# Starting an expert's first products inside the preceding expert, and its biases as two float32r parts

## Chip, cores, metric

One core of a Trainium2 chip runs the whole program. The metric is the device time of one execution in microseconds; the time of the kernel is the median of its runs. The engines are named as in the profile: PE is TensorE (PEld its weight loads), DVE VectorE, ACT ScalarE, POOL GpSimd; SP is the engine that issues most transfers.

## What is computed

Two transformer blocks on 256 tokens of width 1024, in float32. The first has a token mixer of two recurrent branches and then a mixture of 32 experts; the second has attention and a dense feed-forward part. The change is in the experts. Each token goes to its 4 best experts of 32, and what each expert computes is:

```python
gu = xb @ w_gu[e] + b_gu[e]
glu = jnp.minimum(gu[:, :D_EXPERT], SWIGLU_LIMIT)
lin = jnp.clip(gu[:, D_EXPERT:], -SWIGLU_LIMIT, SWIGLU_LIMIT)
act = glu * jax.nn.sigmoid(SWIGLU_ALPHA * glu) * (lin + 1.0)
return (act @ w_down[e] + b_down[e]) * p[:, None].astype(h.dtype)
```

`w_gu[e]` is 1024 x 2048 and `w_down[e]` 1024 x 1024, so an expert reads 12.58 MB of weights, and the 32 experts 402.7 MB.

## The kernel before

The experts run one after the other, over all 32, each with room for 64 tokens (`CAP`). An overflow path, `over`, runs for experts with more tokens; it is a branch that stands behind expert 30.

**Weights.** `moe` lists all 384 chunks of 1 MB in the order of their use: for each expert eight gate/up chunks (128 rows of `w_gu`), then four down chunks (256 rows of `w_down`), at L1177 to L1183. They go through a ring of 16 slots (`K.rings`). `load_to` (L1186) issues the next load on SP's queue; the first 16 are issued ahead, during the merge, and from then on the use of one chunk asks for the load of one more, which waits until the slot it falls on has been read.

**One expert** (`expert`, L1289). `biases(e)` (L1277) takes the two PSUM banks `pg` and `pl` (two buffers each), has POOL spread a selecting pattern `se`, and starts the accumulation with two float32 products of `se` and the bias table `bgu`. Then come the eight gate/up chunks (L1298): the 64 tokens are the stationary operand, the weights move, and each bank takes two half-width products, one in partitions 0 to 63 and one in 64 to 127. A float32 product is two instructions in the trace, so a chunk is eight and the biases are four. `expert_act` (L1219) computes the activation on DVE and ACT from both banks; `act_T` (L1231) transposes its result on PE (L1234) and ACT copies it out (L1236); then the four down chunks (L1309) accumulate in `po`, and DVE scales the result (L1317).

**Between the experts.** Every second expert gathers the tokens of the next pair (`gather`, L1242, products at L1261) and combines an earlier pair into the output (`combine`, L1319, products at L1339). Expert 1's own gather is the rest of the generator `g0`, run behind expert 0.

**Order.** The order in which the code is written is not the order on an engine: the framework's scheduler puts each engine's instructions in a row, within the data dependencies, and only a few are pinned (`issue_after`, `keep_in_program_order`). All SP transfers stand in one queue in their order of issue.

**Constants.** `route_consts` (L1056), during the merge, loads the router's weights, the bias tables and index rows by POOL's queue. `split` (L48) makes a high and a low float32r part of a float32 tile, with a copy on ACT and a subtraction on DVE (L49, L50); the merge's weights go through it, too, and are multiplied in three float32r products each (L76 to L78).

Of the kernel before, what the change touches and what calls it, by code (L numbers as in the profile page):

```python
# [7 lines left out]
F32 = mybir.dt.float32  # L8
# [7 lines left out]
P = 128  # L16
# [1032 lines left out]
NE = 32  # L1049
CAP = 64  # L1050

COMBINE = {e: [(e - 3, e - 2)] for e in range(3, 30, 2)}
COMBINE.update({30: [(28, 29), (30,)], 31: [(31,)]})


def route_consts(K, rc):  # L1056

    nc, I = K.nc, K.I
    def bank():
        return K.psum.tile([P, 512], F32, name="mod", bufs=1)  # L1060
    post_vecs(K, rc, bank)
    wr = rc.tile([P, 8, NE], F32, name="wr")
    nc.gpsimd.dma_start(wr, I["w_router"].rearrange("o (k p) e -> p (o k) e", p=P))
    br = rc.tile([P, NE], F32, name="br")
    bcast_rows(nc, nc.gpsimd, br, I["b_router"], NE)
    bgu = rc.tile([P, 512], F32, name="bgu")
    for q in range(4):
        nc.gpsimd.dma_start(bgu[q * NE:(q + 1) * NE, :], I["b_gu"][0, :, q * 512:(q + 1) * 512])
    bdn = rc.tile([P, 512], F32, name="bdn")
    for q in range(2):  # L1070
        nc.gpsimd.dma_start(bdn[q * 64:q * 64 + NE, :], I["b_down"][0, :, q * 512:(q + 1) * 512])
    iof = rc.tile([P, 256], F32, name="iof")
    nc.gpsimd.iota(iof, pattern=[[1, 256]], base=0, channel_multiplier=0, allow_small_or_imprecise_dtypes=True)
    ups = rc.tile([P, P], F32, name="ups")
    nc.vector.tensor_sub(ups, K.upT, K.ident)

    sel = rc.tile([P, NE, 2], F32, name="sel")
    ih = K.ident.rearrange("p (i h e) -> p i e h", i=2, h=2)
    nc.vector.tensor_add(sel, ih[:, 0], ih[:, 1])
    pb = bank()  # L1080
    for k in range(8):
        nc.tensor.matmul(pb[:, :NE], K.sh2c[:, k:k + 1].to_broadcast([P, P]), wr[:, k, :], start=(k == 0), stop=(k == 7))
    nc.vector.tensor_add(br, pb[:, :NE], br)
    K.rc = wr, br, bgu, bdn, iof, ups, sel


class router:


    def __init__(self, K, rc, psum, mp):  # L1090
        self.K, self.nc, self.rc, self.psum, self.mp = K, K.nc, rc, psum, mp

        def T(name, *shape, dt=F32):
            return rc.tile([P, *shape], dt, name=name)
        self.lg, self.m8, self.idx, self.idf = T("lg", 2, NE), T("top", 2, 8), T("idx", 2, 8, dt=U32), T("idf", 2, 8)
        self.A, self.slot, self.Pw, self.ps = T("A", 2, NE), T("slot", 2, NE), T("Pw", 2, NE), T("ps", 2)
        self.eq, self.rs2 = T("eq", 2, 4, NE), T("rs2", 2)
        self.cnt, self.cmax = T("cnt", NE + 1, dt=I32), T("cmax", 1)
        self.pl = psum.tile([P, 512], F32, name="po", bufs=1)
        self.pc = psum.tile([P, 512], F32, name="tr", bufs=1)  # L1100
        self.h2T = [mp.tile([P, 8, P], F32, name="xT", bufs=2) for _ in range(2)]
# [25 lines left out]
    def top(self, t):  # L1127
        K, nc, lg, A = self.K, self.nc, self.lg[:, t, :], self.A[:, t, :]
        _, br, _, _, iof, _, _ = K.rc
        nc.vector.scalar_tensor_tensor(lg, self.pl[:, t * NE:(t + 1) * NE], self.rs2[:, t:t + 1], br, op0=OP.mult, op1=OP.add)  # L1130
        nc.vector.max(out=self.m8[:, t, :], in_=lg)
        nc.vector.max_index(out=self.idx[:, t, :], in_max=self.m8[:, t, :], in_values=lg)
        nc.vector.tensor_copy(self.idf[:, t, :], self.idx[:, t, :])
        nc.vector.tensor_tensor(self.eq[:, t], iof[:, None, :NE].to_broadcast([P, 4, NE]),
                                self.idf[:, t, :4, None].to_broadcast([P, 4, NE]), op=OP.is_equal)
        return nc.vector.tensor_reduce(A, self.eq[:, t].rearrange("p j e -> p e j"), axis=mybir.AxisListType.X, op=OP.add)

    def count(self):
        K, ups = self.K, self.K.rc[5]
# [26 lines left out]
def moe(K, rc, dbg=None):  # L1166
# [10 lines left out]
    wq = {}  # L1177
    chunks = []
    for e in range(NE):
        for k in range(8):  # L1180
            chunks.append((e, "gu", k))
        for k in range(4):
            chunks.append((e, "dn", k))  # L1183
    nload = [0]
# [57 lines left out]
    def gather(g):  # L1242

        S = mp.tile([P, 2, 2, CAP], F32, name="S", bufs=2)
        SP = mp.tile([P, 2, 2, CAP], F32, name="SP", bufs=1)
        xT = mp.tile([P, 8, 2, CAP], F32, name="xT", bufs=2)
        xTs[g] = xT
        for e0, e1 in ((0, 1), (1, 2)) if g == 0 else ((0, 2),):
            m = e1 - e0
            for t in range(2):  # L1250
                nc.vector.tensor_tensor(S[:, t, e0:e1], iof[:, None, :CAP].to_broadcast([P, m, CAP]),
                                        slot[:, t, g * 2 + e0:g * 2 + e1, None].to_broadcast([P, m, CAP]), op=OP.is_equal)
            if (g, e0) == (0, 0):
                R.scaled(0, 1)
                R.scaled(1, 1)
            for k4 in range(2):
                p = tr() if g else psum.tile([P, 512], F32, name="y", bufs=2)
                for kk in range(4):
                    for t in range(2):
                        k = k4 * 4 + kk  # L1260
                        nc.tensor.matmul(p[:, kk * P:kk * P + m * CAP], h2[:, t, k * P:(k + 1) * P],  # L1261
                                         S[:, t, e0:e1].rearrange("p e c -> p (e c)"), start=(kk == 0 and t == 0),
                                         stop=(kk == 3 and t == 1), skip_group_check=True)
                nc.scalar.activation(xT[:, k4 * 4:k4 * 4 + 4, e0:e1],
                                     p.rearrange("p (k e c) -> p k e c", k=4, e=2)[:, :, :m], AF.Copy)
            if e0 == 0:
                yield
        w = mp.tile([P, 2, P], F32, name="PwT", bufs=3)
        PwT[g] = w
        for t in range(2):  # L1270
            nc.vector.tensor_mul(SP[:, t], S[:, t], Pw[:, t, g * 2:g * 2 + 2, None].to_broadcast([P, 2, CAP]))
        p = tr()
        for t in range(2):
            nc.tensor.transpose(p[:, t * P:(t + 1) * P], SP[:, t].rearrange("p e c -> p (e c)"), K.ident)
        nc.scalar.activation(w, p[:, :2 * P].rearrange("p (t n) -> p t n", t=2), AF.Copy)

    def biases(e):  # L1277

        pg = psum.tile([P, 512], F32, name="pg", bufs=2)
        pl = psum.tile([P, 512], F32, name="pl", bufs=2)  # L1280
        se = mp.tile([P, 2, CAP], F32, name="se", bufs=2)
        nc.gpsimd.tensor_copy(se, sel[:, e, :, None].to_broadcast([P, 2, CAP]))  # L1282
        for i, pp in enumerate((pg, pl)):
            q = slice(i * 2 * NE, (i + 1) * 2 * NE)
            nc.tensor.matmul(pp, se[q].rearrange("p h c -> p (h c)"), bgu[q, :], start=True, stop=False,  # L1285
                             skip_group_check=True)
        return pg, pl

    def expert(e):  # L1289
        xT = xTs[e // 2][:, :, e % 2, :]  # L1290
        pg, pl = accs.pop(e) if e in accs else biases(e)
        for k in range(8):
            w = wq.pop((e, "gu", k))
            load_to(nload[0] + 1)
            for pp, off in ((pg, 0), (pl, 1024)):
                for half in range(2):
                    hs = slice(half * CAP, (half + 1) * CAP)
                    nc.tensor.matmul(pp[hs, :], xT[:, k, :], w[:, off + half * 512:off + half * 512 + 512],  # L1298
                                     start=False, stop=(k == 7), skip_group_check=True)
        b = expert_act(pg, pl)  # L1300
        aT = act_T(b)
        po = psum.tile([P, 512], F32, name="po", bufs=1)
        for k2 in range(4):
            w = wq.pop((e, "dn", k2))
# [49 lines left out]
    R.weights()  # L1354
    for e in range(NE):
        expert(e)
        if e == 0:
            for _ in g0:
                pass
        if e == 30:  # L1360

            K.ahead = {}
# [14 lines left out]
def over(K, mp, psum, tr, expert_act, act_T, cnt, slot, Pw, iof, add_y):  # L1377
# [4 lines left out]
    with tc.If(m > CAP):  # L1382
        with tc.tile_pool(name="over", reuse_waits="tile", bufs=1) as vp:
            with tc.For_i(0, NE) as e:
                n = nc.values_load(cnt[0:1, bass.ds(e, 1)], min_val=0, max_val=256)
                with tc.If(n > CAP):
                    se = vp.tile([P, 2, 2], F32, name="se")
                    nc.vector.tensor_copy(se[:, :, 0:1], slot[:, :, bass.ds(e, 1)])
                    nc.vector.tensor_copy(se[:, :, 1:2], Pw[:, :, bass.ds(e, 1)])
                    for b in range(1, 4):  # L1390
                        S = vp.tile([P, 2, CAP], F32, name="S")
                        SP = vp.tile([P, 2, 2, CAP], F32, name="SP")
                        for t in range(2):
                            nc.vector.tensor_scalar(S[:, t], iof[:, b * CAP:(b + 1) * CAP], se[:, t, 0:1], None, op0=OP.is_equal)
                            nc.vector.tensor_scalar(SP[:, t], S[:, t, None, :].to_broadcast([P, 2, CAP]), se[:, t, 1:2], None,
                                                    op0=OP.mult)
                        xT = vp.tile([P, 8, CAP], F32, name="xT")
# [595 lines left out]
```

## Time and profile before

| | us |
|---|---|
| median of 3 runs (2106.03 to 2109.7) | 2108.91 |
| profiled execution | 2117.05 |
| its span, first to last instruction | 2115.4 |
| PE busy in the span | 1923.3 |
| experts' gate/up products, first to last start | 766.3 to 1726.9 |

The profile is one execution. Its rows give start and length in microseconds from the span's start. Busy time is a share of the whole span, over stages with different limits; what a stage is worth is read in that stage alone. Matmuls overlap, so a row's length includes the drain of its last one. An idle time in brackets names what ended it.

### The profile page before, as it was taken

The numbers are of one execution on the slowest core, as the hardware profiler recorded it, in microseconds if no ns is written. First come the engines' busy times: TensorE is split into PE (matmuls) and PEld (weight loads), VectorE is DVE, ScalarE is ACT, GpSimd is POOL, SyncE is SP. The second block draws the span as 40 slices with busy tenths as digits, with TensorE's granted clock in tenths as the row PEclk, the third lists the DMA queues.
The fourth block names the chain that finished last, engine by engine and source line by source line (L and its number), as shares of the span: only waits on it lengthen the run. The fifth ranks groups of instructions, "written<-read, shape, count | busy, mean of one in ns | idle before, by whom it ended". The sixth has DMA issues, their size and how long they took to land. (4 is left out here: it accounts for less than half of the span.)

```text
span 2115.4 us, 27709 instructions
## 1 busy us (share of the span) xinstructions
PE 1923.3 (91%) x10742; PEld 1167.0 (55%) x10743; DVE 968.4 (46%) x2244; ACT 652.4 (31%) x1368; POOL 172.6 (8%) x247
## 2 busy tenths in 40 slices
PE   4786979799998999999999999999999889998998
PEld 1664758688986763333333233333333328778997
DVE  2797785866464642221122212111221127667777
ACT  2564555476554410000000000000000004564554
POOL 1342131311102000000000000000000000000000
PEclk8798999898999989999999999999999988998999
DMA  8346654447534789999999999999999963333551
GB/s 259 70 124 205 201 158 100 113 111 205 175 127 164 271 322 404 417 389 417 418 417 416 417 412 416 417 418 418 417 416 417 418 231 123 126 120 100 189 189 41
DMA packets 191938, 569.59 MB, mean 269 GB/s; under 512 B 47919, under 2 KB 90776, under 8 KB 158650
## 3 DMA queue, kind: packets, MB, share of 16 engines
q1 hardware_dynamic: 160064, 507.19, 62.4%
q0 software_dynamic: 13392, 47.72, 7.4%
q10 hardware_dynamic: 18346, 12.86, 2.5%
q8 instruction: 86, 1.41, 0.3%
q14 instruction: 50, 0.41, 0.1%
HBM read 555.22 MB, written 12.50 MB: 268 GB/s over the span
## 5 line engine op out<-in xcount | busy, mean ns | idle before, releaser
L1298 PE MATMUL pg<-w,xT 128*64 128x512 f32 x1024 | 358.3, 600 | 0.0
L1298 PE MATMUL pl<-w,xT 128*64 128x512 f32 x1024 | 352.4, 594 | 0.0
L50 DVE TENSOR_TENSOR wlo<-w,whi 128x1024 fp32r<-128x1024 f32 (+1 forms) x185 | 224.1, 1212 | 137.7 <-ACT whi L49 134.8
L49 ACT ACTIVATE whi<-w 128x1024 fp32r<-128x1024 f32 (+1 forms) x189 | 197.3, 1047 | 213.5 <-PE pj L77 68.5
L1309 PE MATMUL po<-w,aT 128*64 128x512 f32 x1024 | 242.2, 617 | 21.3 <-ACT aT L1236 21.3
L1224 ACT ACTIVATE th<-ga 128x512 f32<-128x512 f32 x32 | 20.2, 631 | 639.2 <-DVE ga L1222 639.2
L1317 DVE TENSOR_TENSOR o<-po,g 64x512 f32<-64x512 f32 x64 | 44.1, 689 | 315.2 <-PE po L1309 314.5
L1222 DVE TENSOR_SCALAR ga<-pg 128x512 f32<-128x512 f32 x32 | 22.1, 692 | 355.7 <-PE pg L1298 355.7
L1298 PEld LDWEIGHTS pl<-w,xT 128*64 128x64 f32 x1024 | 104.2, 137 | 146.2 <-issue 146.1
L1298 PEld LDWEIGHTS pg<-w,xT 128*64 128x64 f32 x1024 | 99.2, 137 | 150.0 <-issue 147.5
L1309 PEld LDWEIGHTS po<-w,aT 128*64 128x64 f32 x1024 | 71.2, 141 | 150.7 <-issue 118.0
L77 PE MATMUL pj<-wlo,hh 128*128 128x256 f32 x384 | 116.6, 304 | 3.6 <-DVE wlo L50 3.3
L76 PE MATMUL pj<-whi,hh 128*128 128x256 f32 x384 | 115.4, 300 | 3.8 <-ACT whi L49 3.8
L78 PE MATMUL pj<-whi,hl 128*128 128x256 f32 x384 | 115.0, 299 | 0.0
L76 PE MATMUL pj<-hh,whi 128*128 128x512 f32 (+1 forms) x264 | 100.7, 383 | 11.8 <-ACT hh L49 9.4
L372 DVE SCALAR_TENSOR_TENSOR acc<-padl,taps,acc 128x256 f32<-128x256 f32 x192 | 106.1, 567 | 9.7 <-ACT acc L365 7.6
L78 PE MATMUL pj<-hh,wlo 128*128 128x512 f32 (+1 forms) x264 | 99.6, 378 | 7.1 <-DVE wlo L50 6.9
L77 PE MATMUL pj<-hl,whi 128*128 128x512 f32 (+1 forms) x264 | 100.5, 381 | 0.1
L77 PEld LDWEIGHTS pj<-wlo,hh 128*128 128x128 f32 x384 | 78.3, 204 | 12.0 <-DVE wlo L50 4.5
L1339 PE MATMUL y<-o,PwT 128*128 128x512 f32 (+1 forms) x136 | 72.1, 639 | 13.7 <-DVE o L1317 10.2
L1282 POOL COPY se<-sel 128x128 f32<-128x128 f32 x32 | 12.2, 382 | 868.5 <-PE pl L1285 812.0
L1217 DVE TENSOR_TENSOR x<-x,y 128x512 f32<-128x512 f32 x68 | 46.5, 688 | 78.2 <-PE y L1339 78.2
(676 smaller groups left out, 3615.3 us busy)
## 6 DMA issues: line engine op xcount, KB each, us to landing
w<-in_w_gu_dram SPq DMA_DIRECT2D x256, 1024.0 KB, 11.3
w<-in_w_down_dram SPq DMA_DIRECT2D x139, 1024.0 KB, 13.2
w<-in_w_in_dram POOLq DMA_DIRECT2D x72, 512.0 KB, 5.6
w<-in_w_mod_dram SPq DMA_DIRECT2D x48, 512.0 KB, 6.1
w<-in_w_up_dram SPq DMA_DIRECT2D x22, 1024.0 KB, 5.1
w<-in_w_in_dram SPq DMA_DIRECT2D x8, 1024.0 KB, 5.2
gbc<-gD ACTq DMA_DIRECT2D x16, 256.0 KB, 6.2
actD<-la ACTq DMA_DIRECT2D x16, 256.0 KB, 5.4
```

The source lines that it names most:

```text
L49: K.nc.scalar.activation(hi, src, AF.Copy)
L50: (lo_eng or K.nc.vector).tensor_sub(lo, src, hi)
L76: nc.tensor.matmul(out, ah, bh, start=first, stop=False, **kw)
L77: nc.tensor.matmul(out, ah, bl, start=False, stop=False, **kw)
L78: nc.tensor.matmul(out, al, bh, start=False, stop=last, **kw)
L372: eng.scalar_tensor_tensor(al, pl[:, dy:dy + 4, dx:dx + 64], w, al, op0=OP.mult, op1=OP.add)
L1217: nc.vector.tensor_add(y[:, t, ds_], y[:, t, ds_], p)
L1222: nc.vector.tensor_scalar(a, pg, 7.0, None, op0=OP.min)
L1298: nc.tensor.matmul(pp[hs, :], xT[:, k, :], w[:, off + half * 512:off + half * 512 + 512], start=False, stop=(k == 7), skip_group_check=True)
L1309: nc.tensor.matmul(po[dh * CAP:(dh + 1) * CAP, :], aT[:, k % 4, (k // 4) * CAP:(k // 4 + 1) * CAP], w[:, kk * 1024 + dh * 512:kk * 1024 + ...
L1317: nc.vector.tensor_mul(outs[e // 2][e % 2 * CAP:(e % 2 + 1) * CAP, dh * 512:(dh + 1) * 512], po[hs], K.g2[hs])
L1339: nc.tensor.matmul(ps[dh], PwT[g][hs, t, :], outs[g][hs, dh * 512:(dh + 1) * 512], start=(g > 0), stop=True)
```

## The change

`chunks` lists the first two gate/up chunks of expert e + 1 ahead of expert e's down chunks, so they are loaded in that order. `expert` is split: `up(e, ks)` does the biases, if they aren't done, and the products of the chunks `ks`. `expert(e)` does its own chunks 2 to 7, calls the activation, then does chunk 0 of expert e + 1, the transposes, chunk 1 of expert e + 1, and the down products. Experts 0 and 31 (`ALONE`) aren't started early. The rest of `g0` runs inside each call, which has an effect in expert 0 only.

The bias table is loaded into a buffer of the `la` tag of another pool, split into float32r parts `bgh` and `bgl`, and each bank gets two float32r products in place of a float32 one; `se` is float32r too. To make room, `iof` shrinks from 256 columns to 64 and `eq` loses its token index; `over` subtracts 64 from the slots per block in place of reading further along `iof`.

```diff
+ALONE = 0, 31
...
-    bgu = rc.tile([P, 512], F32, name="bgu")
+    bgu = K.wsp.tile([P, 512], F32, name="la", bufs=2)
     for q in range(4):
         nc.gpsimd.dma_start(bgu[q * NE:(q + 1) * NE, :], I["b_gu"][0, :, q * 512:(q + 1) * 512])
+    bgh, bgl = (rc.tile([P, 512], F32R, name=n) for n in ("bgh", "bgl"))
+    split(K, bgu, bgh, bgl)
...
-    iof = rc.tile([P, 256], F32, name="iof")
-    nc.gpsimd.iota(iof, pattern=[[1, 256]], base=0, channel_multiplier=0, allow_small_or_imprecise_dtypes=True)
+    iof = rc.tile([P, CAP], F32, name="iof")
+    nc.gpsimd.iota(iof, pattern=[[1, CAP]], base=0, channel_multiplier=0, allow_small_or_imprecise_dtypes=True)
...
-        for k in range(8):
+        for k in range(0 if e in ALONE else 2, 8):
             chunks.append((e, "gu", k))
+        if e + 1 < NE and e + 1 not in ALONE:
+            chunks += [(e + 1, "gu", 0), (e + 1, "gu", 1)]
         for k in range(4):
             chunks.append((e, "dn", k))
...
-        se = mp.tile([P, 2, CAP], F32, name="se", bufs=2)
+        se = mp.tile([P, 2, CAP], F32R, name="se", bufs=2)
         nc.gpsimd.tensor_copy(se, sel[:, e, :, None].to_broadcast([P, 2, CAP]))
         for i, pp in enumerate((pg, pl)):
             q = slice(i * 2 * NE, (i + 1) * 2 * NE)
-            nc.tensor.matmul(pp, se[q].rearrange("p h c -> p (h c)"), bgu[q, :], start=True, stop=False,
-                             skip_group_check=True)
+            for j, part in enumerate(bgu):
+                nc.tensor.matmul(pp, se[q].rearrange("p h c -> p (h c)"), part[q, :], start=(j == 0), stop=False,
+                                 skip_group_check=True)
         return pg, pl
...
-    def expert(e):
+    def up(e, ks):
+
         xT = xTs[e // 2][:, :, e % 2, :]
-        pg, pl = accs.pop(e) if e in accs else biases(e)
-        for k in range(8):
+        if e not in accs:
+            accs[e] = biases(e)
+        pg, pl = accs[e]
+        for k in ks:
             w = wq.pop((e, "gu", k))
             load_to(nload[0] + 1)
...
-        b = expert_act(pg, pl)
+
+    def expert(e):
+
+        up(e, range(0 if e in ALONE else 2, 8))
+        ahead = e + 1 < NE and e + 1 not in ALONE
+        b = expert_act(*accs.pop(e))
+        for _ in g0:
+            pass
+        if ahead:
+            up(e + 1, (0,))
         aT = act_T(b)
+        if ahead:
+            up(e + 1, (1,))
         po = psum.tile([P, 512], F32, name="po", bufs=1)
...
         expert(e)
-        if e == 0:
-            for _ in g0:
-                pass
```

## Rows read from the trace of the kernel before

**Rows 1.** The page: GB/s moved by DMA in 40 equal slices.

```profile
GB/s 259 70 124 205 201 158 100 113 111 205 175 127 164 271 322 404 417 389 417 418 417 416 417 412 416 417 418 418 417 416 417 418 231 123 126 120 100 189 189 41
```

**Rows 2.** Stretches: us, busy (x) of PE, PEld, DVE, ACT, POOL, clock, DMA share, GB/s.

```profile
768.00:805.00 37.00, 37.00 (x194) 17.99 (x192) 7.19 (x15) 3.96 (x8) 0.00 (x0) 0.98 0.93 371
...
900.00:930.00 30.00, 28.88 (x134) 11.60 (x136) 6.50 (x12) 2.81 (x5) 0.37 (x1) 1.00 1.01 378
...
1000.00:1200.00 200.00, 189.35 (x812) 66.98 (x814) 39.99 (x67) 12.70 (x22) 2.46 (x7) 0.99 1.02 417
1200.00:1400.00 200.00, 189.87 (x834) 68.10 (x832) 39.21 (x65) 13.33 (x23) 2.56 (x7) 1.00 1.01 415
1400.00:1600.00 200.00, 190.99 (x848) 69.48 (x846) 37.96 (x64) 13.69 (x24) 2.20 (x6) 1.00 1.02 417
```

**Rows 3.** Waits of the DMA queue, 1000 to 1600 us: total, times, longest.

```profile
SPq L1191 <- PE po L1309: 207.4, 80, 6.8
```

**Rows 4.** Last gate/up load of experts 8 and 30: issue, landing time, products.

```profile
991.02 0.33 SPq L1191 DMA_DIRECT2D w<-in_w_gu_dram  x1
...
w<-in_w_gu_dram SPq DMA_DIRECT2D x1, 1024.0 KB, 8.9
...
1025.77 1.03 PE L1298 MATMUL pg<-w,xT 128*64 128x512 f32 x4
1026.63 1.03 PE L1298 MATMUL pl<-w,xT 128*64 128x512 f32 x4
...
1655.50 0.33 SPq L1191 DMA_DIRECT2D w<-in_w_gu_dram  x1
...
w<-in_w_gu_dram SPq DMA_DIRECT2D x1, 1024.0 KB, 10.6
...
1686.62 1.03 PE L1298 MATMUL pg<-w,xT 128*64 128x512 f32 x4
```

**Rows 5.** Timeline of PE, experts 24 to 26.

```profile
1494.14 1.08 PE L1298 MATMUL pg<-w,xT 128*64 128x512 f32 x4
...
1541.84 1.09 PE L1285 MATMUL pg<-bgu,se 64*128 64x512 f32 x2
1542.60 1.12 PE L1285 MATMUL pl<-bgu,se 64*128 64x512 f32 x2
1544.13 0.66 PE L1234 MATMUL tr<-ident,gb 128*128 128x128 f32 x4 [0.40 <-DVE gb L1228]
1545.47 7.09 PE L1309 MATMUL po<-w,aT 128*64 128x512 f32 x32 [0.69 <-ACT aT L1236]
...
1554.40 1.08 PE L1298 MATMUL pg<-w,xT 128*64 128x512 f32 x4
```

**Rows 6.** Timeline of PE in the merge, float32r products.

```profile
676.19 0.39 PE L76 MATMUL pj<-whi,yT0h 128*128 128x512 f32 x1
...
676.41 0.39 PE L77 MATMUL pj<-wlo,yT0h 128*128 128x512 f32 x1
```

**Rows 7.** Expert 30's end: timeline of PE; one stretch, columns as in rows 2.

```profile
1690.91 1.09 PE L1234 MATMUL tr<-ident,gb 128*128 128x128 f32 x4 [2.41 <-DVE gb L1228]
1692.68 9.52 PE L1309 MATMUL po<-w,aT 128*64 128x512 f32 x32 [0.69 <-ACT aT L1236]
...
1714.84 1.08 PE L1298 MATMUL pg<-w,xT 128*64 128x512 f32 x4
...
1690.80:1697.60 6.80, 6.01 (x16) 2.19 (x18) 0.00 (x0) 0.60 (x1) 0.00 (x0) 0.50 1.01 412
```

**Rows 8.** The borrowed buffer's users, the bias loads, the first weight split.

```profile
L921 ACT ACTIVATE la<-oa x16: 292/296/312, 576.5 to 582.8; 128x128 f32<-128x128 f32 x16
...
666.48 1.50 POOL L1068 DMA_DIRECT2D bgu<-in_b_gu_dram  x3 [0.83 <-DMA gt<-actD]
...
bgu<-in_b_gu_dram POOLq DMA_DIRECT2D x4, 64.0 KB, 6.5
...
672.29 1.06 ACT L49 ACTIVATE whi<-w 128x1024 fp32r<-128x1024 f32 x1 [0.46 <-PE pj L78]
```

More of the change, by code (lines that the diff above doesn't have):

```diff
@@ L1083, in route_consts @@
     nc.vector.tensor_add(br, pb[:, :NE], br)
-    K.rc = wr, br, bgu, bdn, iof, ups, sel
+    K.rc = wr, br, (bgh, bgl), bdn, iof, ups, sel
 class router:
@@ L1096, in __init__ @@
         self.A, self.slot, self.Pw, self.ps = T("A", 2, NE), T("slot", 2, NE), T("Pw", 2, NE), T("ps", 2)
-        self.eq, self.rs2 = T("eq", 2, 4, NE), T("rs2", 2)
+        self.eq, self.rs2 = T("eq", 4, NE), T("rs2", 2)
         self.cnt, self.cmax = T("cnt", NE + 1, dt=I32), T("cmax", 1)
@@ L1133, in top @@
         nc.vector.tensor_copy(self.idf[:, t, :], self.idx[:, t, :])
-        nc.vector.tensor_tensor(self.eq[:, t], iof[:, None, :NE].to_broadcast([P, 4, NE]),
+        nc.vector.tensor_tensor(self.eq, iof[:, None, :NE].to_broadcast([P, 4, NE]),
                                 self.idf[:, t, :4, None].to_broadcast([P, 4, NE]), op=OP.is_equal)
-        return nc.vector.tensor_reduce(A, self.eq[:, t].rearrange("p j e -> p e j"), axis=mybir.AxisListType.X, op=OP.add)
+        return nc.vector.tensor_reduce(A, self.eq.rearrange("p j e -> p e j"), axis=mybir.AxisListType.X, op=OP.add)
     def count(self):
@@ L1250, in gather @@
             for t in range(2):
-                nc.vector.tensor_tensor(S[:, t, e0:e1], iof[:, None, :CAP].to_broadcast([P, m, CAP]),
+                nc.vector.tensor_tensor(S[:, t, e0:e1], iof[:, None, :].to_broadcast([P, m, CAP]),
                                         slot[:, t, g * 2 + e0:g * 2 + e1, None].to_broadcast([P, m, CAP]), op=OP.is_equal)
@@ L1390, in over @@
                     for b in range(1, 4):
+                        nc.vector.tensor_scalar(se[:, :, 0:1], se[:, :, 0:1], float(CAP), None, op0=OP.subtract)
                         S = vp.tile([P, 2, CAP], F32, name="S")
@@ L1393, in over @@
                         for t in range(2):
-                            nc.vector.tensor_scalar(S[:, t], iof[:, b * CAP:(b + 1) * CAP], se[:, t, 0:1], None, op0=OP.is_equal)
+                            nc.vector.tensor_scalar(S[:, t], iof, se[:, t, 0:1], None, op0=OP.is_equal)
                             nc.vector.tensor_scalar(SP[:, t], S[:, t, None, :].to_broadcast([P, 2, CAP]), se[:, t, 1:2], None,
```

## The prediction

> **What bounds the kernel now.** I read the page first: from the 16th of the 40 slices to the 32nd the weights come in at 389 to 418 GB/s, nearly always 416 to 418 [rows 1]. That stretch is the 32 experts. The question is whether TensorE or the transfers set its pace, so I cut it into stretches [rows 2]. PE is busy 189 to 191 us of each 200. But from 900 us on the share of the DMA engines is 1.01 or 1.02 as well, and from 1000 us on the rate is 415 to 417 GB/s. From 900 to 930 us it is 378 GB/s at the same full share, so the engines were slow there and not idle. Up to 805 us, at a share of 0.93, they lacked work. The weights therefore already come as fast as this trace ever shows them coming.
>
> Yet PE hardly waits for them. The waits of the DMA queue itself end on PE matmuls (the longest group is in [rows 3]): a load is issued when a product has read its ring slot. How far ahead the loads are is read from one load of an expert. Expert 8's last gate/up chunk is issued at 991.02, lands 8.9 us later at 999.9, and is multiplied from 1025.77: a lead of 25.9 us. Expert 30's is issued at 1655.50, lands at 1666.1 and is multiplied from 1686.62: a lead of **20.5 us** [rows 4]. So PE sets the pace, but it outruns the loads by (25.9 - 20.5) / 22 = 0.25 us per expert and lives on a stock that shrinks. Both paces agree: two experts take PE 1554.40 - 1494.14 = 60.26 us, 30.13 each [rows 5], and an expert's twelve loads, 12.58 MB, at the mean 416.3 GB/s of the last three stretches of [rows 2] take 30.23 us. The two limits lie 0.1 us apart.
>
> **The change, part by part.**
>
> *The two waits per expert.* After its last gate/up product PE does the next expert's biases, waits 0.40 us for the activation, transposes, and waits 0.69 us for the copy of the transposes [rows 5]: 1.09 us per expert. The change puts chunk 0 of the next expert, and its biases, before the transposes and chunk 1 behind them. A chunk is eight instructions, 0.86 us per four (1025.77 to 1026.63 [rows 4]), so 1.72 us. The first gap, from the last product to the transposes, is 1544.13 - 1541.84 = 2.29 us and would hold 1.06 + 1.72 us; the second, 0.69 us, would hold 1.72. Both waits go. What is late next inside PE is nothing: the transposes start some 0.5 us later than they could, with PE at work.
>
> *The biases.* Four float32 instructions take from 1541.84 to 1543.72, 1.88 us [rows 5]. That is 0.43 each and a drain of 0.16. Four float32r products of 512 columns, started 0.22 us apart like the merge's [rows 6], take 1.06 with the same drain: **0.82 us less** per expert. Those rows have 128 rows and the bias 64; had the cost stayed at 0.43 us each, this saves nothing.
>
> So PE's work per expert falls by 1.09 + 0.82 = 1.91 us, to 28.2, for the 30 experts that get their start early, 57 us in all. The loads still take 30.23. PE then eats up its lead at 1.9 + 0.25 = 2.2 us per expert and has none left by about expert 12 or 13; from there it waits about 2 us per expert **for the weights**. The gain is the lead that is left today at the end: 20.5 us at expert 30's last gate/up chunk. That it is the same if only one of the two parts works (0.82 * 30 = 25 or 1.09 * 30 = 33, both over 20.5) makes it robust.
>
> *What the loads gain.* The idle engine time up to 805 us is 37 * (1.02 - 0.93) / 1.02 = 3.3 us [rows 2]. Some of it is the time before the first slot is free, which stays; earlier reading of expert 1's first chunks wins part. I take 1.5, between 0 and 3.3. Against that, PE must see the landing before it starts: I take 0.4 us (none measured; 0 to 0.7, the largest hand-over in [rows 5]). The new order of the loads is the new order of use, on the same queue, with the same 16 slots, so it costs nothing by itself.
>
> *Behind expert 30.* Expert 31 starts nothing early, so activation, transposes, down products, the overflow branch and expert 31 follow as now and move as one block. Expert 30's down chunks land 2.52 us apart behind the last gate/up chunk, all four by 10.1 us; its down products begin 1692.68 - 1686.62 = 6.1 us after that chunk and took 9.52 us [rows 7], so the last one does not wait. Expert 31's gate/up chunks have landed 30.2 us behind it; PE begins them 1714.84 - 1686.62 = 28.2 us behind it [rows 7] and needs the last one 12 us later: no wait either.
>
> *The clock.* During 6.8 us of those down products the granted clock was 0.50, 1.2 GHz, after waits of 2.41 and 0.69 us with little between them [rows 7]; in the stretches of [rows 2] it is 0.98 to 1.00, 2.4 GHz. Starved, PE will wait 0.8 us behind each chunk of 1.72. A fall of that length costs PE 3.4 us. While the loads are the bound the spare 2 us per expert take up most of it, and a PE that runs slow waits less. What can be left is one such fall just at the end: 0 to 3.4 us, I take 0, since the stock of landed chunks recovers whenever PE is the slower one. The Trainium skill's page "TensorE: Matmul & The Clock Gate", section "HAM oscillation — how this bites in real kernels", says that matmul bursts shorter than the DMA waits between them fall back to half clock in each round, which speaks against this change; here the bursts are longer than the waits, and no row of before shows the case. By it the sum would lose the 3.4 us.
>
> *Consts and memory.* The bias table now goes through a borrowed buffer, one ACT copy and one DVE subtraction of 128x512. That buffer's last users end about 583 us, the four loads are issued by 668.0 and land 6.5 us on, 674.5 [rows 8]. POOL waits no longer than now. ACT's first weight split stands at 672.29 and takes 1.06 us for 128x1024; if the bias split, half of that, is queued ahead of it, ACT holds it for 674.5 - 672.3 + 0.5 = 2.7 us, and PE behind it. Else it lies beside PE's work and costs nothing. I take 0.5, between 0 and 2.7. The smaller iota and the shared eq tile cost nothing: two short instructions.
>
> **Sum.** 20.5 + 1.5 - 0.4 - 0.5 = **21.1 us**. The profiled execution, 2117.05 us, would become 2096. It lies 8.1 us above the median of 2108.91, and no row says where, so the median becomes **2087.8**. The bounds give a gain from 20.5 - 0.7 - 2.7 - 3.4 = 13.7 to 23.8; with the unplaced 8.1 us, should they lie in the loads of the profiled run alone, up to 32. That is 2077 to 2095.
>
> **The rivals.**
>
> *The loads can go faster.* If 417 GB/s is only what PE asked for, PE keeps its 57 us and the time is 2051. For it: every load is released by PE [rows 3]. Against it: the engines' share is full, and a load lands 8.9 to 10.6 us after its issue while 1 MB takes 2.5, so several queue, and the rate does not rise with it. Chance 0.07, and a slightly higher rate would land between. The Trainium skill's "DMA: Bandwidth & Descriptors", section "Specifications", gives 435 GB/s as the fabric's ceiling and about 358 as a core's share of HBM. The trace disproves the second; by the first an expert's loads would take 28.9 us, an estimate, and nearly all of PE's saving would stay.
>
> *The loads get slower.* Once PE lives hand to mouth, each slow stretch of the loads counts in full, where the lead hides it today. One is there: 378 GB/s at full share, 900 to 930 us [rows 2]. The 356 chunks between the 16 loaded ahead and the end of expert 30 are 373 MB: 897 us at 416.3 GB/s. The gain of 21 us is gone at 406.7 GB/s on average; halfway to that slow stretch, 397 GB/s, they take 940 us and the kernel 2130. Against it: 600 us in a row at 415 to 417. Chance 0.05.
>
> *It doesn't do what it says.* The order on PE is made by a scheduler, which already moved the biases into the gap and left out the next chunk although that had landed 20 us before. If it sorts the early chunks back, and the float32r biases cost the same, nothing changes: 2108.9. Each alone still gives the forecast. Chance 0.08.
>
> **How the numbers follow.** The forecast has 0.80, 2088. The range starts from 2077 to 2095 and is widened on both sides, to 2066 for loads a little faster than traced and to 2099 for a slow stretch or two. A measurement of this kernel tells about 0.2%, 4 us, from no change. Faster: 0.80 + 0.07 = 0.87; same 0.08; slower 0.05.
>
> **What would show it.** In the new profile PE's waits for the activation and the copy are gone from the middle experts; from about 1050 to 1200 us on PE's weight loads wait for w, 30 to 40 us in all; the loads' rate stays 415 to 417 GB/s, and they take longer from issue to landing; the 64x512 bias instructions are near 0.39 us, not 0.59; expert 31 begins about 21 us earlier. It is wrong if the middle experts come 28.2 us apart to the end (loads faster), if the rate drops below 407, or if PE's old waits stand where they were.

## The result, and the profile after

The changed kernel took **2083.6 us** (median of 4 runs, 2080.58 to 2083.91) beside 2108.44 us for the kernel before on the same chip: ratio 0.9873, 95% interval 0.9841 to 0.9905. The prediction, 2088.0 in a range of 2066 to 2099, held; how far each step held is another matter. Medians and ratios here are of executions that agree with one another; one of f32r_alone_pad, of 4590.32 us, is left out.

The profiled execution of after took 2083.65 us (span 2081.9). Its stretches, columns as in [rows 2]:

```profile
768.00:805.00 37.00, 37.00 (x199) 16.82 (x197) 7.10 (x15) 3.85 (x8) 0.00 (x0) 1.00 1.02 417
900.00:930.00 30.00, 28.56 (x140) 11.75 (x142) 5.13 (x10) 3.10 (x6) 0.75 (x1) 1.00 1.01 411
1000.00:1200.00 200.00, 192.18 (x866) 70.78 (x864) 40.91 (x67) 13.94 (x24) 5.31 (x7) 1.00 1.02 417
1200.00:1400.00 200.00, 192.18 (x868) 69.69 (x868) 41.19 (x70) 14.32 (x25) 5.31 (x7) 1.00 1.02 417
1400.00:1600.00 200.00, 188.57 (x830) 66.26 (x828) 42.48 (x68) 12.74 (x22) 4.56 (x6) 1.00 1.02 417
```

The rate of the loads is what it was. PE is busier than in [rows 2] up to 1400 us, and less busy from 1400 to 1600. What the DMA queue waits for has turned over. Its waits from 1000 to 1600 us (total, times, longest):

```profile
SPq L1199 <- DMA w<-in_w_gu_dram: 144.3, 72, 3.2
SPq L1197 <- DMA w<-in_w_down_dram: 134.9, 66, 3.5
SPq L1197 <- PE pl L1308: 66.9, 53, 4.3
```

In [rows 3] the longest group was a product that had to free a slot; now it is an earlier transfer. The same load as in [rows 4], expert 30's last gate/up chunk, its landing time from the view of DMA issues, then its issue and its products from the timeline:

```profile
w<-in_w_gu_dram SPq DMA_DIRECT2D x1, 1024.0 KB, 20.0
```

```profile
1635.08 0.33 SPq L1197 DMA_DIRECT2D w<-in_w_gu_dram  x1
...
1652.65 1.08 PE L1308 MATMUL pg<-w,xT 128*64 128x512 f32 x4 [0.55 <-DMA w<-in_w_gu_dram]
1653.56 1.03 PE L1308 MATMUL pl<-w,xT 128*64 128x512 f32 x4
1655.14 1.08 PE L1308 MATMUL pg<-w,xT 128*64 128x512 f32 x4 [0.56 <-DMA w<-in_w_gu_dram]
```

It lands at 1655.08 and is multiplied 0.06 us later; before, that lead was 20.5 us [rows 4]. Behind each chunk PE waits 0.55 us for the next. On PE's weight loads the two largest groups of waits for w from 780 to 1700 us (total, times, longest) sum to 28 us, 25 of them behind 1500 us:

```profile
PEld pg L1308 <- DMA w<-in_w_gu_dram: 14.6, 21, 1.5
...
PEld po L1330 <- DMA w<-in_w_down_dram: 13.2, 9, 1.6
```

The lead at an expert's last gate/up chunk is 26.4 us at expert 4, 22.1 at 8, 16.2 at 12, 11.8 at 16, 6.0 at 20 and 1.6 at 24: it shrinks by 1.24 us per expert, and PE is starved from expert 24 or 25 on, not from 12 or 13. PE's own pace says the same: the first down products of experts 5 and 13 start at 931.37 and 1163.53, 29.02 us per expert, where 28.2 was forecast. The waits of PE that are left, from 1000 to 1400 us, and the timeline of PE at an odd expert's end and an even one's:

```profile
PE tr L1280 <- ACT xT L1270: 4.8, 7, 0.7
PE tr L1267 <- ACT aT L1242: 4.8, 7, 0.7
PE y L1360 <- DVE o L1338: 4.7, 6, 0.8
```

```profile
1157.88 0.47 PE L1292 MATMUL pg<-bgh,se 64*128 64x512 f32 x1
1158.18 0.39 PE L1292 MATMUL pg<-bgl,se 64*128 64x512 f32 x1
1158.64 0.50 PE L1292 MATMUL pl<-bgh,se 64*128 64x512 f32 x1
1158.98 0.39 PE L1292 MATMUL pl<-bgl,se 64*128 64x512 f32 x1
1159.30 1.08 PE L1308 MATMUL pg<-w,xT 128*64 128x512 f32 x4
1160.21 1.03 PE L1308 MATMUL pl<-w,xT 128*64 128x512 f32 x4
1161.17 0.66 PE L1240 MATMUL tr<-ident,gb 128*128 128x128 f32 x4
1161.76 1.08 PE L1308 MATMUL pg<-w,xT 128*64 128x512 f32 x4
...
1189.51 0.66 PE L1240 MATMUL tr<-ident,gb 128*128 128x128 f32 x4
1190.86 0.71 PE L1267 MATMUL tr<-S,h 128*128 128x128 f32 x4 [0.69 <-ACT aT L1242]
1191.50 1.08 PE L1308 MATMUL pg<-w,xT 128*64 128x512 f32 x4
```

At the odd end both waits are gone, as predicted. At the even end the scheduler put four of the gather's products, which need the transposes' one bank, ahead of chunk 1, and they wait 0.69 us for the same copy that the down products waited for in [rows 5]. Also at the even ends, PE now waits 0.69 us for the gather's copy xT, which it did not in before from 1000 to 1400 us.

### The profile page after: what moved, and what is told of

It is laid out like the page before. It is cut to its first block, busy times and chain, and to the rows that moved or that the text cites. A ratio compares the mean times of both kernels' runs of the same rounds, so it can differ in the third digit from the quotient of the medians.

```text
span 2081.9 us, 27700 instructions
## 1 busy us (share of the span) xinstructions
PE 1898.8 (91%) x10742; PEld 1159.6 (56%) x10743; DVE 965.6 (46%) x2245; ACT 652.5 (31%) x1369; POOL 184.0 (9%) x247
## 5 line engine op out<-in xcount | busy, mean ns | idle before, releaser
L1308 PE MATMUL pg<-w,xT 128*64 128x512 f32 x1024 | 274.4, 605 | 3.5 <-DMA w<-in_w_gu_dram 3.4
L1308 PE MATMUL pl<-w,xT 128*64 128x512 f32 x1024 | 268.1, 593 | 0.0
L1308 PEld LDWEIGHTS pl<-w,xT 128*64 128x64 f32 x1024 | 75.2, 137 | 146.4 <-issue 146.4
L1308 PEld LDWEIGHTS pg<-w,xT 128*64 128x64 f32 x1024 | 65.2, 136 | 139.4 <-issue 115.9
L1228 DVE TENSOR_SCALAR ga<-pg 128x512 f32<-128x512 f32 x32 | 22.1, 691 | 244.8 <-PE pg L1308 244.8
L1288 POOL CAST se<-sel 128x128 fp32r<-128x128 f32 x32 | 22.4, 702 | 828.4 <-PE pl L1292 828.4
L1267 PEld LDWEIGHTS tr<-S,h 128*128 128x128 f32 x480 | 57.9, 191 | 48.6 <-issue 34.9
```

## Experiments

Three kernels leave work out, and their times are read with that in mind: after_no_bias leaves out the gate/up biases of experts 1 to 30; after_11 and before_11 load eleven chunks per expert and use the third down chunk's weights also for the fourth. A pace below is the time from the first down product of expert 5 to that of expert 13, divided by eight.

**before_again**: the kernel before, unedited.

> The kernel before, unchanged, profiled once more. The two profiles already read differ by 6.9 us at the router, ahead of the experts, where the change does next to nothing, and the profiled execution of before lay 8 us over its median. If that is one slow execution, this profile's first gate/up product starts 5 to 7 us earlier than 766.3 us and its time is about 2108. If the change itself made the part ahead of the experts faster, the start stays at 766 and the time near 2117.

It took 2109.68 us (one run, span 2108.0). Its first gate/up product starts at 762.36 us, 3.9 us earlier than in the profile of before, not 5 to 7, so one long execution accounts for only part of the difference. In two stretches its rate was another than in [rows 2]:

```profile
768.00:805.00 37.00, 37.00 (x196) 17.96 (x194) 7.19 (x15) 3.96 (x8) 0.00 (x0) 1.00 1.00 395
...
900.00:930.00 30.00, 28.89 (x140) 11.56 (x138) 5.12 (x10) 2.81 (x5) 0.36 (x1) 1.00 0.97 372
```

Expert 30's last gate/up chunk is issued at 1651.57, lands at 1662.3 and is used at 1682.68: the lead is 20.4 us, as in [rows 4]. The landing and the use:

```profile
w<-in_w_gu_dram SPq DMA_DIRECT2D x1, 1024.0 KB, 10.7
```

```profile
1682.68 1.03 PE L1298 MATMUL pg<-w,xT 128*64 128x512 f32 x4
```

That execution is the one to set against after, since the profile of before has 7.4 us more span: 3.9 of them ahead of expert 1's down products (817.57 and 813.65), 3.4 behind the start of expert 31's.

**order_only**: the new order, with the float32 biases of before.

```diff
...
-            for j, part in enumerate(bgu):
-                nc.tensor.matmul(pp, se[q]..., part[q, :], start=(j == 0), stop=False,
+            nc.tensor.matmul(pp, se[q]..., bgu[q, :], start=True, stop=False,
```

> The changed kernel with the biases as one float32 product per bank again: the new order alone. Supply theory (the loads, 30.2 us per expert, become the bound once PE's lead of about 20 us is used up, and a gain counts only until then): PE's waits fall from 1.49 to about 0.7 us per expert, 0.78 * 30 = 23 us, just about the lead, so 2084 to 2088. PE theory (PE still sets the end, each part adds its own share of the 25 us): by the forecast's own terms 1.09 of 1.91, 14 us, so 2094.

2087.62 us, ratio 0.9875 [0.9823, 0.9927]: the whole gain within the measurement. The pace is 29.11 us, and expert 30's last chunk has a lead of 0.04 us. Of its waits from 1000 to 1400 us, none is for the copy aT:

```profile
PE y L1357 <- DVE o L1335: 5.5, 7, 0.8
PE tr L1265 <- ACT xT L1268: 4.8, 7, 0.7
```

So the order alone takes 30.13 - 29.11 = 1.02 us from an expert, with the new wait for xT in it, and the float32r biases add 0.09.

**after_no_bias**: those biases not multiplied at all.

```diff
-        for i, pp in enumerate((pg, pl)):
+        for i, pp in enumerate((pg, pl) if e in ALONE else ()):
...
-                                     start=False, stop=(k == 7), skip_group_check=True)
+                                     start=(k == 0 and e not in ALONE), stop=(k == 7), skip_group_check=True)
```

> The changed kernel without the bias products of experts 1 to 30 (their biases are left out of the result; chunk 0 opens the banks): 1.42 us less on PE per expert, 43 us in all. Supply theory: the lead is used up earlier, the end stays where the loads put it, 2080 to 2084. PE theory: 2040 to 2045.

2085.2 us, ratio 0.9883 [0.9845, 0.992], 1 us above the forecast of the supply theory: with 0.97 us less per expert (pace 28.05) the time is that of after. PE is only starved earlier: its weight loads wait 40.8 and 36.6 us in the two groups that hold 14.6 and 13.2 above. The loads set the end.

**after_11** and **before_11**: one load in twelve taken away.

```diff
-        for k in range(4):
+        for k in range(3):
             chunks.append((e, "dn", k))
...
-            w = wq.pop((e, "dn", k2))
-            load_to(nload[0] + 1)
+            w = wq[e, "dn", min(k2, 2)]
+            load_to(nload[0] + (k2 < 3))
```

> The changed kernel with eleven loads per expert in place of twelve: the last down chunk is not loaded, its products read the third one's tile again, so PE's work is the same and part of the weights is left out of the result. Supply theory: the loads take 27.7 us per expert, PE at 29.0 is the bound again to the end, and the waits for weights of experts 24 to 30 go: 6 to 8 us less, 2075 to 2078. PE theory (the waits for weights are not what sets the end): 2083, no change.

> The kernel before with the same eleven loads per expert (the same part of the weights left out). Both theories: PE sets the pace there at 30.1 us per expert and never waits for weights, so no change, 2105 to 2110. If it gains more than 4 us, the loads held up the kernel before already.

after_11: 2059.93 us, ratio 0.9752 [0.9712, 0.9792]. before_11: 2105.5 us, ratio 0.9976 [0.9951, 1.0]. Fewer loads are worth 24 us to the kernel after and 5.3 us to the one before, more than the 4 us that the expectation set as the sign of loads that hold up PE. But PE's weight loads wait for w only 0.6 us in before, from 780 to 1700 us; in before_11 the wait for DVE's o is gone from the list, as it is in after_11, and the pace is 29.91 us for 30.13, 0.22 * 29 = 6 us. So the 5.3 us can be put down to the schedule that the edit changed, and the two kernels have different bounds. The queue of after_11 waits for PE again, the rate falls below the full one, and no product waits for w (waits of SP, then of PE, from 1000 to 1600 us; the same stretch):

```profile
SPq L1197 <- PE pl L1308: 237.8, 105, 3.4
...
PE tr L1267 <- ACT aT L1242: 7.5, 11, 0.7
PE tr L1280 <- ACT xT L1270: 6.9, 10, 0.7
```

```profile
1000.00:1600.00 600.00, 583.66 (x2624) 213.28 (x2622) 126.72 (x208) 42.20 (x73) 15.09 (x20) 1.00 1.00 404
```

The size was missed. The edit did two things: it took away the starvation, and it changed the schedule so that PE's wait for DVE's o in the odd experts, 0.79 us, is gone. The pace is 28.59 us where after had 29.02, 0.43 * 29 = 12 us; the starvation is the other half, by subtraction.

**gather_y**: the gather of the later pairs through the y banks, so that it doesn't share the transposes' bank.

```diff
-                p = tr() if g else psum.tile([P, 512], F32, name="y", bufs=2)
+                p = psum.tile([P, 512], F32, name="y", bufs=2)
```

> The changed kernel with the gathers' products in the two banks of y in place of the one bank of the transposes, which should take away the two waits of 0.69 us that are left in every second expert, some 20 us in 15 experts. Supply theory: no change, 2081 to 2084, the loads set the end. PE theory: 2064 to 2070.

2082.98 us, ratio 0.9859 [0.9816, 0.9902]: no difference from after. The pace fell to 28.54 us, but the waits did not go as meant: from 1000 to 1400 us PE still waits 4.8 us for aT and 4.7 for o; the 4.8 for xT are gone. What PE saved was given to the loads.

**over_early**: the overflow branch behind expert 10 instead of behind expert 30, so that expert 31 too starts early.

```diff
+OVER_AT = 10
-ALONE = 0, 31
+ALONE = 0, 11
...
+        if e == OVER_AT:
             over(K, mp, psum, tr, expert_act, act_T, cnt, slot, Pw, iof, add_y)
```

> The changed kernel with the overflow branch behind expert 10 in place of expert 30, so that expert 31 starts inside expert 30 and expert 11 starts alone. Supply theory: the branch's standstill of PE falls where the loads are 20 us ahead and is paid out of that lead; at the end the last down chunk of expert 31, which lands 11.6 us before its use today, is used as it lands: 6 to 10 us less, 2074 to 2078. PE theory: the standstill is only moved, 2082 to 2085.

2076.07 us, ratio 0.9825 [0.9794, 0.9857]. Since its interval overlaps that of after, both ran once more on one chip.

> The changed kernel, unedited, beside the one with the early overflow branch on the same chip, to tell 2083.6 and 2076.07 us apart, whose intervals overlap (ratios 0.9873 and 0.9825). Theory A, the branch costs TensorE and the loads nothing where a lead covers it: this one at ratio 0.986 to 0.989, the other 0.003 to 0.006 lower, in the same order in each pair of runs. Rival B, the difference lies in the clock's phases ahead of the experts and behind expert 31, which vary from run to run: both at one ratio within 0.002.

> As over_early, beside the changed kernel on the same chip. From the first down product of expert 1 to that of expert 31 the first profiles had 888.8 us (after) and 884.0 us (early branch), so Theory A gives 4 to 6 us, a ratio of 0.982 to 0.985; Rival B gives the ratio of the changed kernel within 0.002, with that stretch of 884 us again and the gain lost behind it.

after_same_chip: 2085.11 us, ratio 0.9858 [0.9824, 0.9892]. over_early_same_chip: 2079.48 us, ratio 0.9822 [0.9791, 0.9853]. The early branch is the faster kernel by 7.5 us between the first two jobs and by 5.6 us on one chip, with intervals that overlap each time; in the order of the runs it was the faster one in four pairs of six, not in each. From the first down product of expert 1 to that of expert 31 after took 888.8 and 887.6 us, over_early 884.0 and 884.5; behind it over_early is also shorter by some 4 to 6 us, and why wasn't tried. Ahead of the experts it is longer: expert 1's down products start at 816.88 and 821.67 us, in after at 811.36 and 814.36, so the two profiled executions on one chip take the same (2084.6 and 2083.83 us). Theory A had the direction, and the size in the experts; the difference of the medians is likely but not settled, and a part of it in the clock's phases isn't excluded.

**f32r_alone**: the float32r biases without the new order.

```diff
-ALONE = 0, 31
+ALONE = range(32)
```

> The changed kernel with every expert alone, so with the old order of products and loads: the float32r biases alone. Supply theory: the trace after shows the four products take 1.42 us where they took 1.72, so 0.3 * 32 = 10 us and 2098 to 2100; with order_only the gains add up to over 30 us, more than both parts together give. The forecast's size, 0.82 us per expert, would give 26 us and 2082 to 2086. PE theory: the two gains add up to the 25 us of both together.

2136.51 us, ratio 1.0121 [1.0083, 1.0159]: 27 us **slower** than before, where I had expected it faster. Two more kernels look for the cause. **alone_f32** is f32r_alone with float32 biases; **f32r_alone_pad** issues the first part of each bias twice:

```diff
-            for j, part in enumerate(bgu):
+            for j, part in enumerate((bgu[0], bgu[0], bgu[1])):
-                nc.tensor.matmul(pp, ..., part[q, :], start=(j == 0), stop=False,
+                nc.tensor.matmul(pp, ..., part[q, :], start=(j < 2), stop=False,
```

> The kernel after with every expert alone (the order of products and loads of before) and with the biases of before (float32, one part): control for the 2136.5 us of the same kernel with float32r biases (ratio 1.0121). Theory A, the shorter biases cost the time: the bias products stood inside the wait for the activation, so two float32r parts only lengthen that wait (0.40 to 0.79 us), and the granted clock falls to half for 3.4 to 6.8 us once in every one or two experts: with float32 biases the wait is 0.40 again, the clock is 1.00 from 1000 to 1600, DMA 416 GB/s, and the time 2104 to 2113. Rival B, the rest of the kernel after costs it (the place of the first gather, the loads' order by lists, the layout): the time stays at 2130 to 2140.

> Every expert alone and float32r biases, and the first bias part issued twice in each bank (the second issue overwrites the first): two extra products of 64x512 per expert, about 0.75 us of added TensorE work that gives nothing. Theory A (a short filler lets the clock fall): the wait in front of the transposes shrinks from 0.79 to 0.0 to 0.2 us, the clock stays at 1.00 from 1000 to 1600, and with more work the time falls from 2136 to 2100 to 2110. Theory C, the clock falls for the waits of 0.69 and 0.79 us (aT, y) that stay: the clock stays at 0.95 and the time at 2130 to 2145. Theory D, what costs is the float32r products themselves: 2145 to 2160.

alone_f32: 2113.29 us, ratio 0.9987 [0.9955, 1.0019], so the rest of the kernel after costs nothing in the old order. f32r_alone_pad: 2127.59 us, ratio 1.0069 [1.0041, 1.0096]: it does **more** work than f32r_alone and is faster. The intervals overlap from 1.0083 to 1.0096, but its five runs, 2122.43 to 2131.13 us, all lie below the four of f32r_alone, 2134.88 to 2139.24, and before took longer beside it (2114.88 us, and 2109.1 beside f32r_alone). The end of one expert on PE, and the stretch of 1000 to 1600 us, in alone_f32:

```profile
1115.47 1.09 PE L1289 MATMUL pg<-bgu,se 64*128 64x512 f32 x2
1116.24 1.12 PE L1289 MATMUL pl<-bgu,se 64*128 64x512 f32 x2
1117.76 0.66 PE L1238 MATMUL tr<-ident,gb 128*128 128x128 f32 x4 [0.40 <-DVE gb L1232]
1119.10 7.09 PE L1327 MATMUL po<-w,aT 128*64 128x512 f32 x32 [0.69 <-ACT aT L1240]
```

```profile
1000.00:1600.00 600.00, 571.04 (x2483) 204.18 (x2479) 118.42 (x197) 39.75 (x69) 6.95 (x19) 0.99 1.02 416
```

in f32r_alone_pad:

```profile
1126.38 0.66 PE L1240 MATMUL tr<-ident,gb 128*128 128x128 f32 x4 [0.56 <-DVE gb L1234]
1127.72 7.09 PE L1330 MATMUL po<-w,aT 128*64 128x512 f32 x32 [0.69 <-ACT aT L1242]
```

```profile
1000.00:1600.00 600.00, 566.74 (x2481) 210.51 (x2478) 119.28 (x196) 39.42 (x68) 10.50 (x20) 0.98 1.01 411
```

and in f32r_alone, with a stretch just behind such an end:

```profile
1121.93 0.39 PE L1292 MATMUL pl<-bgl,se 64*128 64x512 f32 x1
1123.12 0.66 PE L1240 MATMUL tr<-ident,gb 128*128 128x128 f32 x4 [0.79 <-DVE gb L1234]
1124.46 8.50 PE L1330 MATMUL po<-w,aT 128*64 128x512 f32 x32 [0.69 <-ACT aT L1242]
```

```profile
1062.50:1065.80 3.30, 3.24 (x8) 1.00 (x10) 0.00 (x0) 0.01 (x1) 0.00 (x0) 0.50 1.03 415
...
1000.00:1600.00 600.00, 562.32 (x2378) 199.95 (x2375) 115.10 (x190) 37.59 (x65) 14.38 (x19) 0.95 1.00 403
```

In all three an expert that meets no fall of the clock takes 30.44 or 29.81 us: the transposes start when the activation is done, and shorter biases in front only lengthen the wait, 0.40, 0.56 or 0.79 us. They save nothing there. But the longer that wait, the oftener the clock is granted at 0.50 (1.2 GHz) behind it and the 0.69 us that follow: 2, 7 and 12 times from 1000 to 1600 us, mean clock 0.99, 0.98 and 0.95. From expert 5 to expert 29 the paces are 30.29, 30.74 and 31.30 us. The slow time is of the size of the difference: a mean of 0.98 over 600 us is a loss of 12 us, and the pad's 30.74 lies 0.61 us over the mean of 30.44 and 29.81, 12 us for 20 experts; for f32r_alone it is 30 against 23; why not all of the slow time counts wasn't tried. So the falls of the clock are what f32r_alone pays for, by size. The result of the pad lies between Theory A (clock 1.00, 2100 to 2110) and Theory C (0.95, 2130 to 2145): the pad shortened the wait by 0.23 us only, and about half of the cost stays. Theory D is refuted, since more float32r products took less time. That the length of the wait brings the falls is argued from the order of three kernels, whose bias products differ as well; it isn't shown apart from them.

## Why the prediction was right, and where its steps were not

**The bound, and the lead as the gain: right.** PE set the pace, with the loads close behind; the change made the loads the bound; the gain was the lead at expert 30's last gate/up chunk. Against before_again that chunk is used 1682.68 - 1655.14 = 27.5 us earlier. 20.4 of it is the lead, and 7.1 is an earlier landing, of which 2.9 stand already ahead of the experts (expert 0's last gate/up load lands at 736.6 and 733.7), less than executions of one kernel differ there (740.2 in the profile of before). From expert 1's first down product to expert 31's both profiles of before take 914.9 us; after takes 888.8, order_only 889.1, after_no_bias 889.2 and gather_y 889.7, at paces from 28.05 to 29.11 us. So how much PE saves doesn't matter once it is over the lead, as the prediction argued; after_11 and before_11 show the bound on either side.

**The stock that shrinks: misread.** The 0.25 us per expert came from two loads. In the profile of before the lead is 25.8 us at expert 8, 25.2 at 12, 26.0 at 16, 24.7 at 24 and 24.1 at 28: nearly flat, and 3.6 us of the fall lie between experts 28 and 30. The load chosen for the sum, expert 30's, was the right one all the same. **Each part alone gives the forecast: half wrong.** The order alone does (order_only); the float32r biases alone, which were to save PE 25 us, made the kernel 27 us slower (f32r_alone), because in the old order they stand in front of a wait.

**What the loads gain: mis-sized.** Forecast 1.5, measured 7.1 - 2.9 = 4.2 us. The step that failed is the reading of [rows 2] that from 900 to 930 us "the engines were slow there and not idle". With the new order that stretch runs at 411 GB/s in after, and the first one of its table at 417. Against before_again that is 37 * (417 - 395) / 417 = 2.0 and 30 * (411 - 372) / 417 = 2.8 us, 4.8 together, which covers the 4.2; 20.4 + 4.2 = 24.6 us, and the medians lie 24.8 apart, the two profiled spans 26.1. From 900 to 930 us the low rate belonged to the order of the loads: 354 to 378 GB/s in the five profiles with the old order and twelve loads, 405 to 416 in the seven with the new one. From 768 to 805 us no such line can be drawn (353 to 395 and 344 to 417). A share of 1.01 didn't mean that nothing was to be won. In the old order the queue pauses for over 5 us between two loads again and again (in before_again from 903.3 to 908.9 and from 916.5 to 921.7 us), in after never for over 4.4 from 800 to 1600; but such pauses stand also where the old order has 417 GB/s, so how a full share and a low rate go together no run here settles. The hand-over from landing to start, taken at 0.4 us, was 0.06.

**The two waits: nearly right.** Forecast 1.09 us per expert, measured 1.02 by the order alone. The nearness is in part luck: from bias to bias the expert with the combine fell from 29.81 to 28.74 us, which is the forecast, but the one with the gather from 30.44 to 29.49 with a new wait of 0.69 us for xT in it, and what made up for that was not looked for. In after half of the second wait came back at the transposes' bank (0.69 us in even experts): the prediction said that nothing is late next inside PE, and had not asked which other products share that bank.

**The biases: mis-sized, and in part given back.** Forecast 0.82 us, from starts 0.22 us apart as in [rows 6]. Bank to next product they take 1159.30 - 1157.88 = 1.42 us; the float32 pair of order_only takes 1135.55 to 1137.37, 1.82. That is 0.40, and 0.69 / 2 of it is lost to the moved wait: 0.09 us of pace is left. The starts are 0.30 to 0.46 us apart. It cost the total nothing, because the gain was capped by the lead.

**Where PE starves: wrong as a result of these.** PE saves 30.13 - 29.02 = 1.11 us per expert and not 1.91, and the 0.25 us that were added to it aren't there. Forecast from expert 12 or 13, with 30 to 40 us of waits; measured from 24 or 25, with 25 us of them.

**Behind expert 30: right.** From that expert's last gate/up chunk to expert 31's first down product PE took 45.8 us in before_again and 45.0 in after: one block, with no wait for weights in it.

**Loads slower, loads faster: neither.** The rate was 417 GB/s over 600 us, as before, also behind 1500 us, where PE waits for the loads and could have taken more. **The clock: right**, with 0 taken out of 0 to 3.4. The granted clock is 1.00 from 762 to 1660 us in one stretch. The rule of the Trainium skill that the prediction weighed ("TensorE: Matmul & The Clock Gate", "HAM oscillation — how this bites in real kernels") concerns bursts shorter than the waits; here bursts of 1.9 us stand against waits of 0.6, and the trace shows no fall in that stretch, so it wasn't put to the test.

**Consts and the 8.1 us.** No product ahead of the experts was seen to wait for the split of the bias table, but executions of the same kernel differ there by as much (expert 1's down products start at 811.36 in after and at 814.36 in after_same_chip), so the 0.5 us is neither shown nor refuted. The profile of before was 7 us longer than before_again, so taking the gain from the median and not from the profiled execution was right.

## What to carry to other kernels

Where PE and the loads run within a few tenths of a microsecond per tile of each other, read the lead of one load along the kernel: the lead left at the last load, with what the loads themselves gain on the way (20.4 and 4.2 us here), is the most that a faster PE can win, and anything beyond it only moves waits from one engine to another. To win more, load less, or bring work that needs no loads into the stretch where there is still lead (over_early, 5.6 us on one chip, with overlapping intervals). A filler in front of a wait is not shortened for gain: only when other work stands in the gap is a cheaper filler worth anything.

## What the runs showed of the hardware that was not expected

- Shortening TensorE's work made the kernel slower. With waits of 0.79 and 0.69 us around four transposes the granted clock was at 0.50 12 times in 600 us, with 0.40 and 0.69 us twice; the one kernel lies 27 us above before, the other at its level. Starved PE, with a wait of 0.55 us behind 1.9 us of products, kept the clock at 1.00 up to 1660 us.
- Four float32r bias products of 64 rows and 512 columns start 0.30 to 0.46 us apart and take 0.39 to 0.50, more than the 0.22 between starts in [rows 6].
- From 900 to 930 us the DMA engines showed a share of 1.01 at 378 GB/s [rows 2] or 0.97 at 372 (before_again), with the new order of the loads 1.01 at 411: the order alone (order_only, 410) makes the difference.
